# A new order of work at the five sub-layer transitions of a hybrid encoder trunk: uL's first half ahead of the residual, silu between the halves of the second tile's uH, last casts ahead of the last silu

## The chip, the cores and the metric

The kernel runs on one core of one Trainium2 chip. The metric is the device time of one execution in microseconds; it is given as the median of three runs. The profile is of one further execution.

## The reference

Two layers, each a SwiGLU FFN, a token mixer and a second FFN, over x of 256 tokens by 1024 features. Every sub-layer ends in a residual, a layer norm, and the next sub-layer begins with a second standardisation and an adaLN shift and scale:

```python
u = modulate(x, shift, scale)            # standardize(x) * (1 + scale) + shift
f = (silu(g) * up) @ w_ffn_out           # g, up = split(u @ w_ffn_in), 1024 -> 2 x 2816
x = layer_norm(ALPHA * x + 0.5 * (1 + gate) * f, ln_g, ln_b)
u = modulate(x, ...)
m = hybrid_mixer(u, ...)                 # SSD heads beside differential attention, one w_in, one w_out
x = layer_norm(ALPHA * x + (1 + gate) * m, ln_g, ln_b)
u = modulate(x, ...)
f = swiglu(u, ...)
x = layer_norm(ALPHA * x + 0.5 * (1 + gate) * f, ln_g, ln_b)
```

## The kernel before

All products with weights are made in float32 precision from pairs: an operand a is split into a high part (a cast to the type fp32r, on ACT) and a low part (the rest, a subtraction on DVE), and each product is three matmuls (high by high, high by low, low by high). Activations u live in `uH` and `uL`, turned so that features lie on partitions; weights are loaded in halves of 128 by 1024 elements into nine `raw` buffers, cast by `hi_step` and completed by `step` (a low part, plus the next load).

The 256 tokens are two tiles of 128. An FFN runs over eleven blocks of 256 hidden columns; the out-products of a block are made one block later, and for the last four blocks those of tile 1 are kept back. Between two sub-layers stands `cross`: it finishes tile 0 (chain `c0`) and tile 1 (chain `c1`), both by the generator `finish`, while PE makes the kept-back out-products of tile 1 and then the first products of the next sub-layer with tile 0. The order there is written out by hand, in one list for each kind of transition: FFN to mixer (twice, layers 0 and 1), mixer to FFN (twice), FFN to FFN (once, between the layers). Within `cross` DVE, ACT and PE keep exactly the order of the program. The tokens of a list:

- `d0` to `d3`: kept-back out-products; `h`: one cast of a weight half (ACT); `l`: one low part of a weight half (DVE).
- `0 mean`, `0 acc`, `0 rstd`, `0 squares`, `0 rstd2`, `0 turn`: stages of tile 0's chain up to that name. `gate` to `mean` is gate and residual (DVE), `acc` the sums of squares (ACT) and the gamma product (DVE), `squares` the residual stream's new value `xs` (two DVE instructions) and the second sums of squares (ACT), `turn` the normalised `xn` (DVE) and its eight transposes `ptp` (PE). The same with 1 for tile 1.
- `0 us`, `0 u`: the first and the second four features of uH by ACT; `0 m0`, `0 m1`: the unsplit value `um` of each half, again by ACT; `0 l0`, `0 l1` (or a bare `0`, which runs the chain to its end): the subtraction that gives that half of uL, by DVE.
- `P23 1 47`: first products of column blocks 2 and 3 with part 1 and feature blocks 4 to 7. Part 0 is uH by high weights, part 1 uL by high weights, part 2 uH by low weights. Column blocks 0 and 1 share one PSUM bank, 2 and 3 another.
- `e`: evacuation of the first bank. Before a mixer it is one copy on ACT; before an FFN it is `evac`: silu on ACT (tile `sga`), then a product on DVE (tile `hfa`).

After `cross`, tile 1's products with the same weights follow (`mm_a` in an FFN); its first needs a PSUM bank which `e` has emptied. Outside `cross` a scheduler orders instructions within each engine by the dependences.

Of the kernel before, what the change touches and what calls it, by code (L numbers as in the profile page):

```python
# [15 lines left out]
AF = mybir.ActivationFunctionType  # L16
# [11 lines left out]
BC = 256  # L28
NB = DFF // BC
# [16 lines left out]
PRE = 2  # L46
MIX_ADA = (0, 0)
FFN_TO_MIX = ("d0,l,h,d1,d2,d3,0 mean,0 acc,0 rstd,h,h,0 squares,h,l,0 rstd2,h,0 turn,1 gate,1 gate,0 us,0 u,1 mean,"
              "1 acc,P01 02 07,l,1 rstd,0 m0,1 squares,P2 0 07,P2 2 03,P3 0 03,0 l0,P01 1 03,P23 1 03,P3 0 47,1 rstd2,0 m1,"
              "1 turn,0,P01 1 47,1 us,1 u,l,P2 2 47,P23 1 47,l,l,e,P3 2 07,1,h,h,h").split(",")  # L50
MIX_TO_FFN = ("l,d0,h,h,d1,d2,d3,0 mean,h,0 acc,0 rstd,0 squares,l,0 rstd2,h,0 turn,1 gate,1 gate,0 us,0 u,1 mean,"
              "1 acc,P01 02 07,l,1 rstd,0 m0,1 squares,h,P2 0 07,P2 2 03,P3 0 03,0 l0,P01 1 03,P23 1 03,P3 0 47,1 rstd2,0 m1,"
              "1 turn,0,P01 1 47,1 us,1 u,l,P2 2 47,P23 1 47,l,l,e,P3 2 07,1,h").split(",")
FFN_TO_FFN = ("h,l,d0,0 mean,d1,0 acc,0 rstd,h,h,d2,d3,0 squares,l,0 rstd2,h,l,h,h,0 turn,1 gate,1 gate,0 us,0 u,1 mean,"
              "1 acc,P01 02 07,l,1 rstd,0 m0,1 squares,P2 0 07,P2 2 03,P3 0 03,0 l0,P01 1 03,P23 1 03,P2 2 47,P3 0 47,"
              "1 rstd2,0 m1,1 turn,0,P01 1 47,1 us,1 u,l,l,e,P23 1 47,P3 2 07,1,h").split(",")
ORDERS = {"x": FFN_TO_MIX, "m": MIX_TO_FFN, "f": FFN_TO_FFN}

MIX = ("st 1,qk 0 1,ev 1 0,rope 0 0,st 1,small,ev 0 1,tqk 0 0,qk 1 1,rope 1 0,ev 1 1,st 1,st 1,st 1,st 2,st 1,"
# [10 lines left out]
def kernel(  # L70
# [44 lines left out]
    V, S, PE = Queue(nc.vector), Queue(nc.scalar), Queue(nc.tensor)  # L115

    def in_order(on, pe=False):
        V.strict = S.strict = on
        PE.strict = on and pe
# [21 lines left out]
    def gps(name):  # L141
        return pgu.tile([P, 512], F32, tag="gu", name=name)
# [7 lines left out]
    def f(ap):  # L150
        return ap.bitcast(F32)
# [6 lines left out]
    def split(src, hi, lo):  # L158
        S.copy(hi, src)
        V.tensor_tensor(lo, src, f(hi), op=ALU.subtract)  # L160
# [26 lines left out]
    pos = {"load": 0, "hi": 0, "lo": 0}  # L187
    raws, tiles, done = {}, {}, {}
# [6 lines left out]
    def issue_loads(upto):  # L195
        while pos["load"] < min(upto, 2 * len(items)):
            n = pos["load"]
            i, h = divmod(n, 2)
            kind, key, src = items[i]
            if kind == "pair":  # L200
                half = src[h].rearrange("(k p) c -> p k c", p=P)
            else:
                half = src.rearrange("(h k p) c -> h p k c", h=2, p=P)[h]
            shape = {"cols": [4, BC], "pair": [4, BC], "adh": [2, 512]}.get(kind, [1, D])
            raw = rp.tile([P] + shape, F32, tag="raw", name=f"raw_{key}_{h}")
            nc.sync.dma_start(raw, half)
            raws[n] = raw[:, 0, :] if shape[0] == 1 else raw
            pos["load"] += 1
# [13 lines left out]
    def hi_step():  # L222
        n = pos["hi"]
        i, h = divmod(n, 2)
        kind, key, _ = items[i]
        if kind in ADA:
            return False
        issue_loads(n + 1)
        shape = [D] if kind == "rows" else [4, BC]
        ht, lt = [wtile(shape, f"{e}{key}_{h}", F32R) for e in "hl"]  # L230
        tiles.setdefault((kind, key), []).append((ht, lt))
        keep(S.copy(ht, raws[n]), "a")
        pos["hi"] += 1
        return True
# [6 lines left out]
    def step(n=1):  # L241
        for _ in range(n):
            k = pos["lo"]
            if k >= 2 * len(items):
                return
            i, h = divmod(k, 2)
            kind, key, _ = items[i]
            issue_loads(k + 1)
            if kind in ADA:
                pos["hi"] = max(pos["hi"], k + 1)  # L250
                {"ada": ada_step, "adh": adh_step}[kind](key, raws.pop(k), h)
            else:
                if pos["hi"] <= k:
                    hi_step()
                ht, lt = tiles[kind, key][h]
                keep(V.tensor_tensor(lt, raws.pop(k), f(ht), op=ALU.subtract), "v")
            pos["lo"] += 1
            issue_loads(k + 1 + AHEAD)

    stream = {}  # L260

    def order(ins, name):
        tc.add_manual_dep(ins.ins, name, mybir.DependencyInfo(
            mybir.DependencyClass.NoSync, mybir.DependencyReason.SCHED_ONLY), reason="order of issue")

    def keep(ins, e):
        stream[e] = ins.ins.name
        q = V if e == "v" else S
        if q.last and not q.strict:
            order(ins, q.last)  # L270

    def upto(kind, key):
        step(done[kind, key] - pos["lo"])
# [5 lines left out]
    def flush():  # L279
        while late:  # L280
            late.pop(0)()
# [225 lines left out]
    def ln_rows(l, s):  # L507
        lg = wtile([D], f"lg{l}_{s}")
        nc.sync.dma_start(lg, ln_g[l, s].partition_broadcast(P))
        lb = wtile([D], f"lb{l}_{s}")  # L510
        nc.sync.dma_start(lb, ln_b[l, s].partition_broadcast(P))
        slb = sm.tile([P, 1], F32, tag="slb", name=f"slb{l}_{s}", bufs=2)
        S.activation(lb, lb, AF.Identity, accum_out=slb)
        return lg, lb, slb
# [96 lines left out]
    def form_b(o, w, j):  # L611
        sl = slice(j * P, (j + 1) * P)
        for kt in range(KT):
            wh, wl = w[kt // 4]
            mm3(o, wh[:, kt % 4, sl], wl[:, kt % 4, sl], uH[:, :, kt, :], uL[:, :, kt, :], kt == 0, kt == KT - 1)
# [24 lines left out]
    class Ffn:  # L640
# [41 lines left out]

        def evac(self, o, name):
            sg = tp.tile([P, BC], F32, tag="sg", name="sg" + name)
            S.activation(sg, o[:, 0:BC], AF.Silu)
            hf = tp.tile([P, BC], F32, tag="hf", name="hf" + name)
            V.tensor_tensor(hf, o[:, BC:2 * BC], sg, op=ALU.mult)
            return hf
# [144 lines left out]
        def blocks(self, nxt):  # L833
            upto("rows", f"o{self.nm}_{0}")
            for b in range(NA - 1):
                for j in range(2):
                    self.out_both(b, j)
            rows = None
            for b in range(NA, NB):
                step(self.mark[b] - pos["lo"])  # L840
                if self.nm == "00" and b == NA + 2:
                    setup_mixer()
                w = self.weights(b)
                self.htile(b)
                if b == NB - 1:
                    rows = ln_rows(self.l, self.s)
                    target = done["rows", f"o{self.nm}_{b}"] + (PRE if nxt else 0)
                else:
                    target = self.mark[b + 1]
                for j in range(2):  # L850
                    step((target - pos["lo"] + 1 - j) // (2 - j))
                    o = gps(f"ob{self.nm}_{b}{j}")
                    form_b(o[:, 0:BC], w[0], j)
                    form_b(o[:, BC:2 * BC], w[1], j)
                    self.out_both(b - 1, j)
                    hf = self.evac(o, f"b{self.nm}_{b}{j}")
                    hH, hL = self.hts[b]
                    split(hf, hH[:, j, :], hL[:, j, :])
                    flush()
            for h in range(2):  # L860
                for j in range(2):
                    self.out_mm(0, NB - 1, j, (h,))
            defer = [lambda b=b: [self.out_mm(1, b, j) for j in range(2)] for b in range(NB - NDEF, NB - 1)]
            defer.append(lambda: [self.out_mm(1, NB - 1, j, (h,)) for h in range(2) for j in range(2)])
            if nxt is None:
                defer = [lambda h=h: [self.out_mm(1, b, j, (h,)) for b in range(NB - NDEF, NB) for j in range(2)]
                         for h in range(2)]
            cross(self.l, self.s, self.accs, rows, nxt, defer)
# [531 lines left out]
```

## Time and profile before

| quantity | value |
|---|---|
| median of three runs | 1075.6 us (1075.52 to 1075.69) |
| the profiled execution | 1074.92 us, of which the span of the trace is 1073.2 us |
| PE busy in the span | 1031.1 us, 96% |
| DVE, ACT, POOL busy | 825.4, 580.9, 36.1 us (77%, 54%, 3%) |
| mean share of the DMA engines by the hardware queue | 69.6% |

PE is busy all along but for the start, the end and short stretches at the five transitions. A wait in a row stands in brackets behind the instruction that ended it, with the instruction that released it.

### The profile page before, as it was taken

The numbers are of one execution on the slowest core, as the hardware profiler recorded it, in microseconds if no ns is written. First come the engines' busy times: TensorE is split into PE (matmuls) and PEld (weight loads), VectorE is DVE, ScalarE is ACT, GpSimd is POOL, SyncE is SP. The second block draws the span as 40 slices with busy tenths as digits, with TensorE's granted clock in tenths as the row PEclk, the third lists the DMA queues.
The fourth block names the chain that finished last, engine by engine and source line by source line (L and its number), as shares of the span: only waits on it lengthen the run. The fifth ranks groups of instructions, "written<-read, shape, count | busy, mean of one in ns | idle before, by whom it ended". The sixth has DMA issues, their size and how long they took to land.

```text
span 1073.2 us, 19053 instructions
## 1 busy us (share of the span) xinstructions
PE 1031.1 (96%) x7433; PEld 944.3 (88%) x7433; DVE 825.4 (77%) x1284; ACT 580.9 (54%) x1046; POOL 36.1 (3%) x79
## 2 busy tenths in 40 slices
PE   4999999989999999999999999999999999999996
PEld 2899999879897899999989999998899879999995
DVE  5788699688998798768588868847899878756454
ACT  3474434378756755343477433536876578535241
POOL 0000000010000100000010000000000010000000
PEclk9999999999999999999999999999999999999998
DMA  9989799948456389879547979883664628866411
GB/s 341 319 298 370 273 306 407 306 138 254 134 188 225 99 304 341 286 294 361 199 138 249 335 296 377 282 280 107 199 209 150 213 91 302 282 221 216 158 41 39
DMA packets 162559, 258.25 MB, mean 241 GB/s; under 512 B 10807, under 2 KB 125983, under 8 KB 162469
## 3 DMA queue, kind: packets, MB, share of 16 engines
q1 hardware_dynamic: 162468, 257.04, 69.6%
q8 instruction: 58, 0.95, 0.4%
q14 instruction: 33, 0.26, 0.1%
HBM read 255.96 MB, written 1.05 MB: 239 GB/s over the span
## 4 chain that ended last, share of the span: by engine, by line
PE 77%; DVE 10%; ACT 7%; issue 3%; DMA 2%; POOL 1%; SPq 0%; DVEq 0%; POOLq 0%; ACTq 0%
PE ob L108 38%; PE acc L108 18%; PE oa L108 5%; PE ocx L108 2%; PE accx L108 2%; PE ovx L108 2%; DVE xs L108 2%; ACT uH L108 2%; ACT um L108 1%; PE oqkx L108 1%; PE ozx L108 1%; ACT junk L108 1%; DVE acc L108 1%; PE pr L108 1%; DVE lg L108 1%
## 5 line engine op out<-in xcount | busy, mean ns | idle before, releaser
L108 PE MATMUL ob<-uH,hg 128*128 128x256 f32 x576 | 162.6, 282 | 0.0
L108 PE MATMUL ob<-uL,hg 128*128 128x256 f32 x576 | 162.2, 282 | 0.0
L108 PE MATMUL ob<-uH,lg 128*128 128x256 f32 x576 | 161.8, 281 | 0.3 <-DVE lg L108 0.3
L108 PE MATMUL ob<-uH,lu 128*128 128x256 f32 x576 | 162.0, 281 | 0.0
L108 PE MATMUL ob<-uH,hu 128*128 128x256 f32 x576 | 161.9, 281 | 0.0
L108 PE MATMUL ob<-uL,hu 128*128 128x256 f32 x576 | 161.7, 281 | 0.0
L108 PE MATMUL acc<-ho,hH 128*128 128x512 f32 x352 | 137.5, 392 | 1.0 <-ACT ho L108 1.0
L108 PE MATMUL acc<-lo,hH 128*128 128x512 f32 x352 | 137.8, 391 | 0.7 <-DVE lo L108 0.7
L108 PE MATMUL acc<-ho,hL 128*128 128x512 f32 x352 | 137.2, 390 | 0.0
L108 ACT ACTIVATE sgb<-ob 128x256 f32<-128x256 f32 x72 | 27.6, 383 | 202.2 <-PE ob L108 201.8
L108 DVE TENSOR_TENSOR lo<-raw_o,ho 128x1024 fp32r<-128x1024 f32 x88 | 105.6, 1220 | 14.4 <-ACT ho L108 7.2
L108 PEld LDWEIGHTS ob<-uH,hg 128*128 128x128 f32 x576 | 108.3, 188 | 6.2 <-issue 2.5
L108 PEld LDWEIGHTS ob<-uH,lu 128*128 128x128 f32 x576 | 110.1, 191 | 1.2 <-issue 1.2
L108 PEld LDWEIGHTS ob<-uH,lg 128*128 128x128 f32 x576 | 110.2, 191 | 0.6 <-DVE lg L108 0.5
L108 PEld LDWEIGHTS ob<-uL,hg 128*128 128x128 f32 x576 | 108.1, 188 | 2.5
L108 DVE TENSOR_TENSOR lg<-raw_g,hg 128x1024 fp32r<-128x1024 f32 x84 | 101.2, 1221 | 11.2 <-ACT hg L108 5.6
L108 PEld LDWEIGHTS ob<-uH,hu 128*128 128x128 f32 x576 | 108.4, 188 | 0.5 <-issue 0.4
L108 PEld LDWEIGHTS ob<-uL,hu 128*128 128x128 f32 x576 | 108.1, 188 | 0.0
L108 DVE TENSOR_TENSOR lu<-raw_u,hu 128x1024 fp32r<-128x1024 f32 x84 | 100.3, 1219 | 3.4 <-PE ob L108 1.7
L108 ACT CAST hg<-raw_g 128x1024 fp32r<-128x1024 f32 x84 | 86.9, 1056 | 28.1 <-PE acc L108 17.8
L108 DVE TENSOR_TENSOR hfb<-ob,sgb 128x256 f32<-128x256 f32 x72 | 30.3, 420 | 91.2 <-ACT sgb L108 91.0
L108 ACT CAST ho<-raw_o 128x1024 fp32r<-128x1024 f32 x88 | 90.2, 1049 | 12.7 <-PE ob L108 9.0
(535 smaller groups left out, 2307.1 us busy)
## 6 DMA issues: line engine op xcount, KB each, us to landing
raw_o<-in_w_ffn_out_dram SPq DMA_DIRECT2D x88, 512.0 KB, 5.8
raw_g<-in_w_ffn_in_dram SPq DMA_DIRECT2D x84, 512.0 KB, 5.6
raw_u<-in_w_ffn_in_dram SPq DMA_DIRECT2D x84, 512.0 KB, 6.1
raw<-in_w_ffn_in_dram SPq DMA_DIRECT2D x8, 512.0 KB, 8.1
lg<-in_ln_g_dram SPq DMA_DIRECT2D x6, 512.0 KB, 6.0
lb<-in_ln_b_dram SPq DMA_DIRECT2D x6, 512.0 KB
raw_qk0x<-in_w_in_dram SPq DMA_DIRECT2D x4, 512.0 KB, 3.6
raw_qk1x<-in_w_in_dram SPq DMA_DIRECT2D x4, 512.0 KB
```

Of the source, the lines that this page charges most:

```text
L108: ins = emit(*args, **kwargs)
```

## The change

Three things move; no arithmetic changes, and no instruction is added or removed.

1. In all three lists `0 l0` (uL's first half of tile 0, DVE) stands ahead of `1 squares` (tile 1's `xs`) where it stood behind it. PE's uH products `P3 0 47` (four matmuls, in the FFN-to-FFN list also `P2 2 47`) move ahead of the first uL products. In the mixer-to-FFN list one cast `h` moves from behind `1 squares` to ahead of `0 turn`.
2. In all three lists `e` moves from behind the low parts of the weights to a place between `1 us` and `1 u`, that is between the two halves of tile 1's uH on ACT, and ahead of the tokens `l` on DVE.
3. In the first FFN alone (`nm == "00"`) all casts and low parts of the last out-weights are asked for before the last block's first half, its last silu is ordered behind the last of these casts, and the two steps for the next sub-layer (`PRE`) come after the last split, from where on the program's order holds.

```diff
-FFN_TO_MIX: ...1 acc,P01 02 07,l,1 rstd,0 m0,1 squares,P2 0 07,P2 2 03,P3 0 03,0 l0,P01 1 03,P23 1 03,P3 0 47,1 rstd2,0 m1,
-            1 turn,0,P01 1 47,1 us,1 u,l,P2 2 47,P23 1 47,l,l,e,P3 2 07,1,h,h,h
+FFN_TO_MIX: ...1 acc,P01 02 07,l,1 rstd,0 m0,0 l0,1 squares,P2 0 07,P2 2 03,P3 0 07,P01 1 03,P23 1 03,1 rstd2,0 m1,
+            1 turn,0,P01 1 47,1 us,e,1 u,l,P2 2 47,P23 1 47,l,l,P3 2 07,1,h,h,h
-MIX_TO_FFN: ...l,0 rstd2,h,0 turn,...,1 rstd,0 m0,1 squares,h,P2 0 07,P2 2 03,P3 0 03,0 l0,P01 1 03,P23 1 03,P3 0 47,1 rstd2,0 m1,
-            1 turn,0,P01 1 47,1 us,1 u,l,P2 2 47,P23 1 47,l,l,e,P3 2 07,1,h
+MIX_TO_FFN: ...l,0 rstd2,h,h,0 turn,...,1 rstd,0 m0,0 l0,1 squares,P2 0 07,P2 2 03,P3 0 07,P01 1 03,P23 1 03,1 rstd2,0 m1,
+            1 turn,0,P01 1 47,1 us,e,1 u,l,P2 2 47,P23 1 47,l,l,P3 2 07,1,h
-FFN_TO_FFN: ...1 rstd,0 m0,1 squares,P2 0 07,P2 2 03,P3 0 03,0 l0,P01 1 03,P23 1 03,P2 2 47,P3 0 47,
-            1 rstd2,0 m1,1 turn,0,P01 1 47,1 us,1 u,l,l,e,P23 1 47,P3 2 07,1,h
+FFN_TO_FFN: ...1 rstd,0 m0,0 l0,1 squares,P2 0 07,P2 2 07,P3 0 07,P01 1 03,P23 1 03,
+            1 rstd2,0 m1,1 turn,0,P01 1 47,1 us,e,1 u,l,l,P23 1 47,P3 2 07,1,h
 evac:
-            S.activation(sg, o[:, 0:BC], AF.Silu)
+            self.silu = S.activation(sg, o[:, 0:BC], AF.Silu)
 blocks:
-                    target = done["rows", f"o{self.nm}_{b}"] + (PRE if nxt else 0)
+                    target = done["rows", f"o{self.nm}_{b}"] + (PRE if nxt and self.nm != "00" else 0)
-                    step((target - pos["lo"] + 1 - j) // (2 - j))
+                    step(target - pos["lo"] if j or (self.nm == "00" and b == NB - 1) else (target - pos["lo"] + 1) // 2)
+                    cast = stream["a"] if j == 0 else cast
                     hf = self.evac(o, f"b{self.nm}_{b}{j}")
+                    ends = self.nm == "00" and b == NB - 1 and j == 1
+                    if ends:
+                        order(self.silu, cast)
+                        in_order(True)
                     split(hf, hH[:, j, :], hL[:, j, :])
+                    if ends:
+                        step(PRE)
```

## Rows read from the trace of the kernel before

**Rows 1.** The page: busy time by engine.

```profile
PE 1031.1 (96%) x7433; PEld 944.3 (88%) x7433; DVE 825.4 (77%) x1284; ACT 580.9 (54%) x1046; POOL 36.1 (3%) x79
```

**Rows 2.** The chain that ended last: start, duration, what.

```profile
390.97 5.65 PE ob L108 x48
```

**Rows 3.** Waits of PE: in total, times, longest, us.

```profile
PE oa L108 <- DVE uL L108: 4.2, 6, 1.4
PE oqkx L108 <- DVE uL L108: 3.6, 4, 1.6
```

**Rows 4.** Timeline, end of the first FFN: start, duration, engine, instruction [idle before].

```profile
212.87 1.99 ACT L108 CAST ho<-raw_o 128x1024 fp32r<-128x1024 f32 x2
...
213.94 2.36 DVE L108 TENSOR_TENSOR lo<-raw_o,ho 128x1024 fp32r<-128x1024 f32 x2 [0.52 <-ACT ho L108]
...
213.97 0.73 PE L108 MATMUL acc<-ho,hH 128*128 128x512 f32 x2 [0.98 <-ACT ho L108]
...
215.72 1.05 ACT L108 ACTIVATE lb<-lb 128x1024 f32<-128x1024 f32 x1
...
220.11 0.69 DVE L108 TENSOR_TENSOR acc<-acc,gate 128x512 f32<-128x512 f32 x1
...
229.21 1.00 DVE L108 TENSOR_SCALAR xn<-xs,nmqp,rmp 128x512 f32<-128x512 f32 x2 [0.69 <-POOL rmp L182]
...
229.90 1.09 PE L108 MATMUL ptp<-ident,xn 128*128 128x128 f32 x8 [0.79 <-DVE xn L108]
```

**Rows 5.** Timeline, first transition from mixer to FFN.

```profile
356.80 2.90 ACT L108 ACTIVATE uH<-ptp,mod 128x128 fp32r<-128x128 f32 x8 [2.96 <-PE ptp L108]
...
361.15 1.48 ACT L108 ACTIVATE um<-ptp,mod 128x128 f32<-128x128 f32 x4
...
362.22 1.41 DVE L108 SCALAR_TENSOR_TENSOR xs<-accx,rp,lb 128x512 f32<-128x512 f32 x2 [0.60 <-POOL rp L182]
...
363.54 0.68 DVE L108 TENSOR_TENSOR uL<-um,uH 128x512 fp32r<-128x512 f32 x1
...
365.68 1.00 DVE L108 TENSOR_SCALAR xn<-xs,nmqp,rmp 128x512 f32<-128x512 f32 x2 [0.69 <-POOL rmp L182]
...
366.74 1.05 PE L108 MATMUL ptp<-ident,xn 128*128 128x128 f32 x8
...
367.38 2.90 ACT L108 ACTIVATE uH<-ptp,mod 128x128 fp32r<-128x128 f32 x8 [0.30 <-PE ptp L108]
...
367.72 1.22 DVE L108 TENSOR_TENSOR lg<-raw_g,hg 128x1024 fp32r<-128x1024 f32 x1
...
368.86 2.36 DVE L108 TENSOR_TENSOR lu<-raw_u,hu 128x1024 fp32r<-128x1024 f32 x2
...
369.00 0.74 PE L108 MATMUL oa<-lg,uH 128*128 128x256 f32 x4
...
370.30 1.28 ACT L108 ACT_TABLE_LOAD   x1
...
372.01 0.42 DVE L108 TENSOR_TENSOR hfa<-oa,sga 128x256 f32<-128x256 f32 x1 [0.79 <-ACT sga L108]
...
372.49 1.21 PE L108 MATMUL oa<-hg,uH 128*128 128x256 f32 x8 [0.48 <-DVE hfa L108]
...
376.12 1.10 PE L108 MATMUL oa<-hu,uH 128*128 128x256 f32 x8
```

**Rows 6.** Timeline, the transition from FFN to FFN.

```profile
564.07 2.35 DVE L108 TENSOR_TENSOR lu<-raw_u,hu 128x1024 fp32r<-128x1024 f32 x2
...
564.62 2.90 ACT L108 ACTIVATE uH<-ptp,mod 128x128 fp32r<-128x128 f32 x8 [1.62 <-PE ptp L108]
...
568.30 1.21 PE L108 MATMUL oa<-hg,uH 128*128 128x256 f32 x8 [0.46 <-DVE hfa L108]
```

**Rows 7.** Busy time by stretch: us (instructions) of PE, PEld, DVE, ACT, POOL; PE clock; DMA.

```profile
20.00:25.00 5.00, 1.02 (x8) 0.97 (x8) 3.39 (x9) 2.54 (x6) 0.00 (x0) 0.80 1.07 398
25.00:30.00 5.00, 4.50 (x20) 3.68 (x20) 4.52 (x5) 3.81 (x5) 0.00 (x0) 0.52 0.97 346
```

More of the change, by code (lines that the diff above doesn't have):

```diff
@@ L48 @@
 FFN_TO_MIX = ("d0,l,h,d1,d2,d3,0 mean,0 acc,0 rstd,h,h,0 squares,h,l,0 rstd2,h,0 turn,1 gate,1 gate,0 us,0 u,1 mean,"
[L49 to L53, printed above, removed]
+              "1 acc,P01 02 07,l,1 rstd,0 m0,0 l0,1 squares,P2 0 07,P2 2 03,P3 0 07,P01 1 03,P23 1 03,1 rstd2,0 m1,"
+              "1 turn,0,P01 1 47,1 us,e,1 u,l,P2 2 47,P23 1 47,l,l,P3 2 07,1,h,h,h").split(",")
+MIX_TO_FFN = ("l,d0,h,h,d1,d2,d3,0 mean,h,0 acc,0 rstd,0 squares,l,0 rstd2,h,h,0 turn,1 gate,1 gate,0 us,0 u,1 mean,"
+              "1 acc,P01 02 07,l,1 rstd,0 m0,0 l0,1 squares,P2 0 07,P2 2 03,P3 0 07,P01 1 03,P23 1 03,1 rstd2,0 m1,"
+              "1 turn,0,P01 1 47,1 us,e,1 u,l,P2 2 47,P23 1 47,l,l,P3 2 07,1,h").split(",")
 FFN_TO_FFN = ("h,l,d0,0 mean,d1,0 acc,0 rstd,h,h,d2,d3,0 squares,l,0 rstd2,h,l,h,h,0 turn,1 gate,1 gate,0 us,0 u,1 mean,"
-              "1 acc,P01 02 07,l,1 rstd,0 m0,1 squares,P2 0 07,P2 2 03,P3 0 03,0 l0,P01 1 03,P23 1 03,P2 2 47,P3 0 47,"
-              "1 rstd2,0 m1,1 turn,0,P01 1 47,1 us,1 u,l,l,e,P23 1 47,P3 2 07,1,h").split(",")
+              "1 acc,P01 02 07,l,1 rstd,0 m0,0 l0,1 squares,P2 0 07,P2 2 07,P3 0 07,P01 1 03,P23 1 03,"
+              "1 rstd2,0 m1,1 turn,0,P01 1 47,1 us,e,1 u,l,l,P23 1 47,P3 2 07,1,h").split(",")
 ORDERS = {"x": FFN_TO_MIX, "m": MIX_TO_FFN, "f": FFN_TO_FFN}
```

## The prediction

> **What bounds the kernel now.** I read the page first: PE is busy for 1031.1 of 1073.2 us [rows 1], so what can be won is PE's waiting. The view of PE's waits says where it is: the products with uL wait for DVE, 4.2 us before FFNs and 3.6 us before mixers [rows 3]. In order of time these are two waits at each transition: one for uL's first half of tile 0 (1.0 to 1.6 us, 6.0 us over the five) and one for tile 1's uL (0.2 to 0.5 us). The three transitions into an FFN add a wait for `hfa` of 0.2 to 0.5 us [rows 5, 6], and the end of the first FFN adds waits for the last out-weights and for `xn` [rows 4]. All of it is some 11 us, 1%. The chain of waits, and then the timeline of each transition, show what stands behind: DVE and ACT work through tile 1's chain (`xs`, sums, `xn`, uH, um, uL) while PE fills the time with tile 0's products. So the question at each place is whether PE or tile 1's chain comes last.
>
> That is read at `ptp`, tile 1's eight transposes. Where PE waited for `xn`, the transposes began 0.69 us after its start, 229.21 to 229.90 [rows 4]. In the first mixer-to-FFN transition `xn` starts at 365.68, so PE could have transposed from 366.37 and did so at 366.74 [rows 5]: a reserve of 0.37. The same pair of rows stands in all five transitions and gives, in their order, 0.37, 0.37, 0.75, 0.37 and 0.09 us. A wait taken out ahead of `ptp` is therefore worth at most 2.0 us in all, not 6.0; the rest becomes a wait for `xn`.
>
> **Part 1, uL's first half ahead of `xs`.** A product occupies PE for 0.118 us (5.65 us for 48) [rows 2], so the four moved ones cover 0.47 us, the eight 0.94, and they are as long where they are taken away. The subtraction takes DVE some 0.61 us from start to next start and needs `um`, which ACT ends at 361.15 + 1.48 = 362.63; `xs` was free to start at 362.22 [rows 5]. DVE works in order, so `xs` now waits behind the subtraction until 362.65 + 0.61 = 363.27, and with it the sums, `rstd2` and `xn` come 1.05 us later. The five transitions, by the same two rows: 0.4, 1.05, 0.75, 1.1 and 0.8 to 1.05 us. Less the reserve, `ptp` comes 0.05, 0.7, 0.0, 0.75 and 0.7 us later than before, although PE has finished the uL products earlier. The cast moved ahead of `0 turn` falls where ACT stood idle for 2.96 us [rows 5] and costs nothing; without that cover it is 0.95 us on tile 0's uH. It frees ACT for the second `um`, which then no longer holds the second half of uL; that one now follows `xn`.
>
> **Part 2, silu amid uH.** Before a mixer `e` is one copy on ACT. It needs the first bank, which PE ends shortly before the first half of uH is done; um comes at the same distance as before. I add 0.25 us for uL's second half behind `xn`, and carry on to tile 1: +0.3 us (layer 0) and +1.0 us (layer 1).
>
> Before an FFN `e` also puts `hfa` into DVE's order, and behind it now stand `l,l,l`, the low parts that PE's `P2 2 47` and `P3 2 07` need; behind those stand tile 1's uL. Before, they ran while ACT made uH: lg at 367.72, the two lu from 368.86, and only then `hfa` at 372.01 [rows 5]. Walked forward for the first mixer-to-FFN transition: uH starts at 367.38 + 0.7 = 368.05, its first half takes 1.45 (half of 2.90), so 369.5; the table load of 1.28 stands in front of silu, 370.8; silu to `hfa` is 0.43 (371.58 to 372.01), 371.25; `hfa` holds DVE 0.34, 371.6; lg 1.13, and PE may start `P2 2 47` at 372.85, where it started at 369.00. PE has nothing else: its order is fixed too, and the first bank is done by 369.6. Then lu twice, 375.0; the last four products 375.1 to 375.6; tile 1's first product at 375.6 instead of 372.49, that is 3.1 us later. Of this, what tile 1 lost behind it comes back: from 372.49 to 376.12 stand 24 products, 2.83 us, and two transposes, 0.25, so 0.55 us of waiting for uL that has time now. Net +2.55 us. If tile 1's chain were not late (part 1 harmless) it would be +1.9; +2.8 if nothing came back but half. The second mixer-to-FFN transition has the same rows and the same sum.
>
> Between the FFNs silu needs no table load: uH from 564.62, unchanged by the 0.0 above, silu after PE's first bank at 566.2, `hfa` to 567.0, lu twice to 569.25 where they were done at 566.4 [rows 6]; last products to 569.85, against 568.30 for tile 1's first product: +1.55, less 0.55 that comes back, +1.0 us (0.3 to 1.5).
>
> Here a rule speaks against the change. The load of 1.28 us at 370.30 is followed by `hfa` 0.43 us after its end [rows 5], so nothing stands between load and silu. The Trainium skill (ScalarE: Activation LUTs, What ACT_TABLE_LOAD costs) gives a switch of tables 1.28 us and a drain of 1.38 more. By that page silu would come 1.4 us later still in the two transitions and the sum be 2.8 us higher; this trace shows no drain, and I follow the trace.
>
> **Part 3, the last casts.** Before, both casts stood behind the last silu on ACT, at 212.87, both low parts followed from 213.94, and PE waited at 213.97 [rows 4]. The casts go to ACT's idle stretch ahead of that silu, and the low parts to DVE's beside them; the loads that wait for their `raw` buffers start earlier by as much, behind the two layer-norm loads on SP. DVE's order behind the last split is then three low parts, first the two of `PRE`, where it was five. Two low parts and their wait, 2 x 1.14 + 0.5, bring tile 0's gate product from 220.11 to 217.35; if the activation of `lb` at 215.72 (1.05 us) stays between the casts, to 218.1. `xn` follows, and PE, whose own waits there (0.98 and its followers) vanish too, starts the transposes 2.0 to 2.75 us before 229.90. I take 2.2, nearer to the case in which `lb` stays. Should ACT take `lb` ahead of the last silu, its load would hold both, and 0.6 us would be left of it.
>
> **The sum.** FFN to mixer, layer 0: -2.2 + 0.3 = -1.9; mixer to FFN: 2 x 2.55 = +5.1; FFN to FFN: +1.0; FFN to mixer, layer 1: +1.0. In all +5.2 us. The blocks behind each transition hold PE without a wait, so nothing there takes it up. Against the profiled execution's 1074.92 us that is 1080.1; the median of the runs is 0.7 us above that execution, so 1080.8. From the bounds (first FFN, first mixer's transition, mixer to FFN, FFN to FFN, second mixer's): -2.75 + 0.05 + 3.8 + 0.3 + 0.3 = +1.7 at the one end, -0.6 + 0.3 + 5.6 + 1.5 + 1.1 = +7.9 at the other: 1077.3 to 1083.5 for this case.
>
> **Rivals.** *The silu does no harm* (the low parts are not late for PE, because DVE takes them ahead of `hfa` after all, or has done them before). For it: DVE had 0.79 us idle ahead of `hfa`. Against it: their order in the program, which DVE kept in every row of `cross`. Then only part 1's lateness is left: 0.65 for each mixer-to-FFN transition, 0.25 between the FFNs, 1.0 and -1.9: +0.65, or 1076.3.
>
> *Faster.* Tile 1's chain is not the bound, and PE's waits go as meant. It decides at `xn`: it would have to start about 1 us earlier than part 1 puts it, `um` being ready before `xs` may start. Then up to 2.0 us of reserve are won, 2.2 at the first FFN and the 1.1 us of waits for `hfa`: 1070.5. The rows of `um` against `xs` speak against it.
>
> *The clock falls.* Waits of over 3 us with little PE work around them come up only in the two mixer-to-FFN transitions of the changed kernel. Once before, PE did 1.02 us of work in 5 us, and the granted clock went from 1.0 to 0.5, 2.4 to 1.2 GHz, and stayed there over the next 4.5 us of products (0.52) [rows 7]: 4.5 x 0.48 = 2.2 us a fall, so 1083.0 or 1085.2. Against it: there are some 2 us of products just ahead. The Trainium skill (TensorE: Matmul & The Clock Gate, HAM oscillation) tells of the same: waits between bursts put the clock down, and the next burst starts at half speed; rows 7 agree.
>
> **Chances.** A measurement here tells apart some 0.2%, 2.15 us: slower is above 1077.8, faster below 1073.4. The forecast has 62 in 100, the fall of the clock 18, the harmless silu 12, faster 8. So slower 0.80 (the first two), same 0.12, faster 0.08. The range: from under the harmless silu, 1075.5, up to one fall of the clock with some late terms, 1084.0; faster and two falls are left out, some 15 in 100.
>
> **What will show it.** Right: `lg` and `lu` behind `hfa` on DVE in three transitions, PE's waits there now for `lg` and `lu` (3 us once in each mixer-to-FFN transition), waits for `xn` ahead of `ptp`, no wait for `ho`, gate product of the first FFN at 217 to 218 us, and PE's busy time unchanged. Wrong: `xn` no later than before against `um`, or `l` ahead of `hfa`; a clock below 1.0 at a transition would be the third rival.

## The result and the profile after

The changed kernel takes 1084.2 us (median of 4 runs, 1082.3 to 1085.1) where the kernel before takes 1075.6 on the same chip: 1.0083 times as long, 95% interval 1.0064 to 1.0101. A second series gave 1082.4 us (6 runs) against 1074.75, 1.0073 (1.0059 to 1.0088). The forecast was slower, 1080.8, range up to 1084.0: the sign came, the size was 1.6 to 3.4 us short, and the first median lies just above the range.

The page of the changed kernel answers to [rows 1] with this line (busy us, share of the span of 1083.1 us, instructions), and the view of PE's waits to [rows 3] with those under it:

```profile
PE 1036.7 (96%) x7433; PEld 950.8 (88%) x7433; DVE 824.7 (76%) x1284; ACT 581.0 (54%) x1046; POOL 38.4 (4%) x79
```

```profile
PE ptp L108 <- DVE xn L108: 10.4, 6, 1.9
...
PE oa L108 <- DVE hfa L108: 3.6, 2, 2.2
...
PE acc L108 <- ACT hH L108: 1.8, 1, 1.8
```

The waits for uL are gone from the top, as meant. In their place stand waits for `xn` ahead of tile 1's transposes and for `hfa`, and one for `hH` that the forecast did not have. PE's busy time has grown by 5.6 us although no product was added: some of its products ran at the lower clock.

The turns are named here in their order: x0 (FFN to mixer, layer 0), m0 (mixer to FFN), f (FFN to FFN), x1, m1. In the timeline of m0, which answers to [rows 5], start, duration, engine, instruction and, in brackets, the idle time before it read:

```profile
364.40 0.69 DVE L108 TENSOR_TENSOR uL<-um,uH 128x512 fp32r<-128x512 f32 x1 [1.07 <-ACT um L108]
365.01 1.40 DVE L108 SCALAR_TENSOR_TENSOR xs<-accx,rp,lb 128x512 f32<-128x512 f32 x2
...
368.47 1.00 DVE L108 TENSOR_SCALAR xn<-xs,nmqp,rmp 128x512 f32<-128x512 f32 x2 [0.69 <-POOL rmp L182]
369.16 1.24 PE L108 MATMUL ptp<-ident,xn 128*128 128x128 f32 x8 [1.85 <-DVE xn L108]
...
371.35 1.28 ACT L108 ACT_TABLE_LOAD   x1
...
372.64 0.38 ACT L108 ACTIVATE sga<-oa 128x256 f32<-128x256 f32 x1
372.93 1.50 ACT L108 ACTIVATE uH<-ptp,mod 128x128 fp32r<-128x128 f32 x4
373.06 0.42 DVE L108 TENSOR_TENSOR hfa<-oa,sga 128x256 f32<-128x256 f32 x1 [2.99 <-ACT sga L108]
373.40 1.22 DVE L108 TENSOR_TENSOR lg<-raw_g,hg 128x1024 fp32r<-128x1024 f32 x1
373.54 2.07 PE L108 MATMUL oa<-hg,uH 128*128 128x256 f32 x8 [1.34 <-DVE hfa L108]
...
374.53 2.35 DVE L108 TENSOR_TENSOR lu<-raw_u,hu 128x1024 fp32r<-128x1024 f32 x2
375.41 1.48 PE L108 MATMUL oa<-lg,uH 128*128 128x256 f32 x6
```

DVE's order is the forecast's: uL, then `xs`, then `xn`, and `hfa` ahead of `lg` and `lu`. DVE stands idle for 2.99 us in front of `hfa` with `lg` behind it. The silu starts 0.01 us after the load of the table: of the drain that the Trainium skill puts behind it (ScalarE: Activation LUTs, What ACT_TABLE_LOAD costs) this trace shows nothing either. PE's row at 373.54 is what the forecast did not have: these are tile 1's products with the high parts, which PE takes before `lg` is there. So within `cross` PE keeps the order of the list among the list's own products only: these, which the program has behind `cross`, came in between. Eight of them last 2.07 us where [rows 5] has 1.21.

The busy time by stretch (columns as in [rows 7]) shows why:

```profile
360.00:370.00 10.00, 8.14 (x71) 7.93 (x69) 7.01 (x18) 7.53 (x22) 2.43 (x5) 1.00 0.17 53
370.00:377.00 7.00, 5.66 (x28) 5.25 (x27) 4.01 (x6) 6.97 (x18) 0.00 (x0) 0.52 0.17 50
...
762.00:770.00 8.00, 7.33 (x39) 6.99 (x39) 5.71 (x12) 6.51 (x18) 0.00 (x0) 0.57 0.61 184
...
895.00:899.00 4.00, 4.00 (x23) 3.95 (x22) 3.90 (x6) 3.82 (x10) 0.00 (x0) 0.58 0.58 184
```

The third column from the end is the granted clock: 0.52 to 0.58 over the three stretches behind m0, x1 and m1, so for most of each it stood at the lower of its two levels, 1.2 GHz. By the clock's record in the trace that was 6.83, 6.83 and 3.41 us. The text calls such a stretch a fall of the clock. The profile of the kernel before has none at a turn.

The end of the first FFN, which answers to [rows 4]:

```profile
213.62 0.39 ACT L108 ACTIVATE sgb<-ob 128x256 f32<-128x256 f32 x1 [3.74 <-PE ob L108]
...
216.56 1.06 ACT L108 ACTIVATE lb<-lb 128x1024 f32<-128x1024 f32 x1 [2.56 <-DMA lb<-in_ln_b_dram]
...
217.62 0.39 ACT L108 CAST hH<-hfb 128x256 fp32r<-128x256 f32 x1
...
218.06 0.50 PE L108 MATMUL acc<-ho,hH 128*128 128x512 f32 x1 [1.77 <-ACT hH L108]
...
222.40 0.69 DVE L108 TENSOR_TENSOR acc<-acc,gate 128x512 f32<-128x512 f32 x1
...
232.25 1.08 PE L108 MATMUL ptp<-ident,xn 128*128 128x128 f32 x8 [1.64 <-DVE xn L108]
```

The casts of `ho` are done ahead of the last silu as meant. But ACT now takes the pass over `lb` between silu and the copy `hH`, waits 2.56 us there for the transfer of `lb`, and PE waits 1.77 us for `hH`.

### The profile page after: what moved, and what is told of

The parts are those of the page before. It is cut to its first block, busy times and chain, and to the rows that moved or that the text cites. A ratio compares the mean times of both kernels' runs of the same rounds, so it can differ in the third digit from the quotient of the medians.

```text
span 1083.1 us, 19061 instructions
## 1 busy us (share of the span) xinstructions
PE 1036.7 (96%) x7433; PEld 950.8 (88%) x7433; DVE 824.7 (76%) x1284; ACT 581.0 (54%) x1046; POOL 38.4 (4%) x79
## 4 chain that ended last, share of the span: by engine, by line
PE 81%; DVE 7%; ACT 6%; issue 2%; DMA 2%; POOL 1%; SPq 0%; DVEq 0%; POOLq 0%; ACTq 0%
PE ob L108 37%; PE acc L108 19%; PE oa L108 6%; PE oqkx L108 3%; PE ocx L108 3%; PE accx L108 2%; PE ovx L108 2%; ACT junk L108 2%; DVE xs L108 1%; ACT uH L108 1%; ACT um L108 1%; PE ozx L108 1%; PE pr L108 1%; DMA lb<-in_ln_b_dram 1%; PE psex L108 1%
```

## The experiments

One table for all runs comes first. Each number is the time that a stretch took in that kernel's profile, less the time in the profile of before, by the starts of PE's rows. The stretches: `start` up to the first FFN's last `ob` product; `FFN1 end` up to x0's first transpose; `mixer 0` up to that mixer's first output product; `m0 ptp` up to tile 1's transposes in m0; `m0 rest` up to the next FFN's first `ob`; `f` up to the `ob` after the turn; `x1 ptp` up to tile 1's transposes in x1; `x1 rest` up to a product `scx` 32 us behind them, inside the second mixer; `m1 ptp` and `m1 rest` like those of m0. `sum` is the difference of the whole spans. The last column has the turns with a fall of the clock, and its us.

```
kernel              start FFN1end mixer0 m0ptp m0rest    f  x1ptp x1rest m1ptp m1rest    sum  falls at turns
after                1.93   0.41  -0.64  0.71  2.09 -0.21  0.16  2.56  0.74  2.16   9.91  m0 6.83, x1 6.83, m1 3.41
e1_part1             1.93   0.00  -0.67  0.71 -0.27 -0.17  0.77  0.03  0.72  0.02   3.05  m0 3.41, m1 3.41
e2_part2             2.53   0.00  -0.86 -0.08  2.35 -0.09  0.00  0.01  0.02  1.89   5.76  m1 3.41
e3_part3             1.79   0.32  -0.93  0.00 -0.03 -0.15  0.00  0.00  0.01  0.01   1.00  x0 3.41
e4_parts12           1.59  -0.01  -0.69  0.70  2.73  0.13  0.77  1.51  0.56  0.63   7.90  m0 3.41, x1 3.41
e5_all               1.68  -0.42  -0.72  0.69  2.55 -0.24  0.76  1.39  0.70  0.65   7.03  m0 6.83, x1 3.41
e6_all_lb            0.43  -2.02  -0.67  0.69  2.45 -0.26  0.15  0.19  0.64  0.62   2.21  none
e7_all_split         0.21   0.82  -0.68  0.69  0.00 -0.25  0.77  2.67  0.65  0.03   4.90  FFN1 end 3.41, x1 6.83
e8_all_warm          0.12  -0.03  -0.65  0.70  2.34 -0.27  0.15  0.09  0.70  0.68   3.81  none
e9_part3_lb         -0.03  -2.02  -0.53  0.02 -0.01 -0.25 -0.61  0.02  0.01  0.02  -3.37  none
e10_part3_lb_split   0.78  -2.03  -0.83  0.00  0.01 -0.29 -0.61  0.03  0.00 -0.23  -3.20  none
e11_all_mended       0.84  -2.00  -0.62  0.71  0.01 -0.22  0.16  0.10  0.59  0.06  -0.38  none
e12_part3_lb_start  -1.27  -2.07   1.94  0.02 -0.01 -0.59 -0.61  0.02  0.02  0.06  -2.51  none (mixer 0 3.41)
```

Three columns carry noise. `start` differs by up to 2.6 us between kernels with the same code there. It goes mostly with the cold stretch at about 22 us, which lasts 6.83 us in before, e6 to e10 and 10.24 us in the others (none in e12). `mixer 0` is 0.5 to 0.9 us shorter than in the one profile of before wherever its clock held, whatever was changed. `x1 ptp` has a third FFN in front of it that took 0.61 us less in seven of the profiles, so 0.15 there is 0.76 of the turn.

**e1, part 1 alone.** The lists get the early `0 l0`, the eight products and the cast; `e` stays. The list into an FFN, for one:

```diff
-... 0 squares,l,0 rstd2,h,0 turn, ... 1 rstd,0 m0,1 squares,h,P2 0 07,P2 2 03,P3 0 03,0 l0,P01 1 03,P23 1 03,P3 0 47,1 rstd2
+... 0 squares,l,0 rstd2,h,h,0 turn, ... 1 rstd,0 m0,0 l0,1 squares,P2 0 07,P2 2 03,P3 0 07,P01 1 03,P23 1 03,1 rstd2
```

> Part 1 alone (uL's first half ahead of xs, the uH products and one cast moved; e and the first FFN as before). Theory order (tile 1's chain is late behind the subtraction, and PE waits for xn ahead of the transposes): ptp is late by 0.05, 0.7, 0.0, 0.75 and 0.7 us in the five transitions, some +2 us in all, PE waiting 1.4 to 1.9 us for xn in each, and the clock stays at 1.0. Theory clock (the waits also put PE's clock to half): in addition falls at two or three transitions at 1.5 to 2.4 us each, +5 us or more. Theory gain (the change's own aim): the 6.0 us of waits for uL go and nothing comes: -5 us.

1077.8 us, 1.0025 (1.0016 to 1.0034). `ptp` is 0.71, 0.77 and 0.72 us late in m0, x1 and m1, and no other column but the noise of `start` is late. The waits are for `xn` (in m0 1.84 us). The lateness of part 1 was forecast at 0.7, 0.75 and 0.7 us. The theory of the clock is half right here: it fell at m0 and m1 for 3.41 us each, but the rests behind, -0.27 and 0.02 us, show no cost.

**e2, part 2 alone.** Only `e` is moved:

```diff
-"1 turn,0,P01 1 47,1 us,1 u,l,P2 2 47,P23 1 47,l,l,e,P3 2 07,1,h"
+"1 turn,0,P01 1 47,1 us,e,1 u,l,P2 2 47,P23 1 47,l,l,P3 2 07,1,h"
```

> Part 2 alone (silu between the halves of tile 1's uH). Theory order as predicted (low parts behind hfa, PE has nothing else to do): +1.9 us in each mixer-to-FFN transition, +1.5 between the FFNs, about 0 before mixers: +5 us. Theory order as amended by the changed kernel's trace (tile 1's high products are put into the wait): 0 to +1.5 us in all. Theory clock: falls only in the mixer-to-FFN transitions, if at all, +1.5 us each.

1079.2 us, 1.0032 (1.0020 to 1.0045). m0 costs 2.35 us with no fall of the clock, m1 1.89 with one, the turns f, x0 and x1 nothing: less than +5 us in all, more than the amended theory allowed. In m0 DVE stands idle 2.73 us in front of `hfa` and PE waits 1.94 us for it.

**e3, part 3 alone.** The first FFN's end as in the change, the lists as before:

```diff
-step((target - pos["lo"] + 1 - j) // (2 - j))
+step(target - pos["lo"] if j or (self.nm == "00" and b == NB - 1) else (target - pos["lo"] + 1) // 2)
...
+if ends:
+    order(self.silu, cast)
+    in_order(True)
```

> Part 3 alone (first FFN). Theory lb (ACT takes the activation of lb ahead of the last copy hH and waits there for lb's load): PE waits some 1.8 us for hH instead of for ho, ptp of the first transition comes 0.5 us later than before, and the total is within 1 us of before. Predicted in its place: 2.2 us faster.

1074.9 us, 0.9996 (0.9987 to 1.0004): the gain of 2.2 us that the forecast gave to part 3 is not there.

**e4, parts 1 and 2 together.** The lists of the change, the first FFN as before.

> Parts 1 and 2 without part 3. If part 3 is worth nothing, this has the changed kernel's time, +8 to +9 us. Theory order alone: +2.5 to +3 us with a clock of 1.0 at all transitions. Theory clock: the difference to that is in stretches at 1.2 GHz, one at each of two to three transitions, and the mean granted clock is 0.984 to 0.988 against 0.994 before.

1080.4 us, 1.0051 (1.0037 to 1.0064), 5.3 us above before, so neither the 8 to 9 of the whole change nor the 2.5 to 3 of the order alone. m0 costs 3.4 us and m1 1.2; x1 has a fall of the clock and takes 1.51 us more behind `ptp`, where e1 has none and takes 0.03.

**e5, the change once more,** beside the three kernels that take one suspect out of it.

> The changed kernel itself, a second time, on one chip with the three kernels below. Two theories of why the three parts together cost more than parts 1 and 2 and part 3 one by one (+5.3 and -0.2 us). Clock theory: the order of work costs as much as in those runs, and the rest is the clock, which falls to its lower level at more transitions when all three parts are in; the profile then shows falls around the transitions beside the one at the start, each worth about 1.5 us per 3.4 us at the lower level, and the time is 1082 to 1085. Rival: the first execution profile was unlucky and the sum is that of the parts, 1080 to 1081, with one fall or none.

1082.4 us, 1.0073 (1.0059 to 1.0088), with falls at m0 and x1. The ten runs of both series lie between 1080.6 and 1085.1, all above e4's median. The mean granted clock was 0.983 to 0.990 in them and 0.988 to 0.992 in e4's: the theory of the clock fits, and the sum of parts alone is too low.

**e6, the change with `lb` out of the way.** In the first FFN `ln_rows` now leaves out ACT's pass over `lb`; the line behind `step(PRE)` makes it instead.

```diff
-rows = ln_rows(self.l, self.s)
+rows = ln_rows(self.l, self.s, self.nm != "00")
...
 if ends:
     step(PRE)
+    S.activation(rows[1], rows[1], AF.Identity, accum_out=rows[2])
```

> The changed kernel with one edit at the end of the first FFN: ACT's pass over lb is issued behind the last casts and can no longer stand between the last silu and the copy hH. Theory (lb is why part 3 won nothing): the gate product of the first FFN's end comes at 217.5 to 218.5 us instead of 222.4 (relative to a start as late as in that profile add up to 1.9), the wait of 1.77 us for hH is gone, tile 0's transposes begin 2 to 4 us earlier than in the changed kernel, and the time is 2 us below e5. Rival: the products gain, but the first mixer gives it back, because its start is set by another engine: its output products are no earlier than in e5 and the time is within 0.5 us of e5. Second rival: xn still waits for lb through the gate and nothing moves at all.

1078.6 us, 1.0037 (1.0024 to 1.0050), 3.8 us below e5. The timeline of the first FFN's end:

```profile
212.12 0.38 ACT L108 ACTIVATE sgb<-ob 128x256 f32<-128x256 f32 x1 [3.74 <-PE ob L108]
...
213.00 0.41 ACT L108 CAST hH<-hfb 128x256 fp32r<-128x256 f32 x1 [0.49 <-DVE hfb L108]
...
215.21 1.05 ACT L108 ACTIVATE lb<-lb 128x1024 f32<-128x1024 f32 x1
...
218.47 0.69 DVE L108 TENSOR_TENSOR acc<-acc,gate 128x512 f32<-128x512 f32 x1
...
228.32 1.08 PE L108 MATMUL ptp<-ident,xn 128*128 128x128 f32 x8 [1.29 <-DVE xn L108]
```

`hH` follows the silu by 0.88 us instead of 4.00, the gate product stands at 218.47, and the stretch is 2.02 us shorter than in before. Nothing takes that up. The order in m0 is still the change's, so this clean profile also shows what follows there:

```profile
369.55 1.32 PE L108 MATMUL oa<-hg,uH 128*128 128x256 f32 x8 [2.20 <-DVE hfa L108]
...
385.33 1.05 ACT L108 CAST hg<-raw_g 128x1024 fp32r<-128x1024 f32 x1 [2.92 <-DMA raw_g<-in_w_ffn_in_dram]
386.28 0.64 ACT L108 CAST hH<-ph 128x256 fp32r<-128x256 f32 x2
...
386.97 0.51 PE L108 MATMUL acc<-ho,hH 128*128 128x512 f32 x1 [1.32 <-ACT hH L108]
```

After m0 ACT has the copies `hH` behind a cast that waits 2.92 us for its weights, and PE waits 1.32 us more, 17 us after the turn. In the kernel before the copies stand ahead of that cast, and PE does not wait; the same stretch of its timeline:

```profile
385.08 0.64 ACT L108 CAST hH<-ph 128x256 fp32r<-128x256 f32 x2
...
386.04 1.05 ACT L108 CAST hg<-raw_g 128x1024 fp32r<-128x1024 f32 x1 [0.31 <-DMA raw_g<-in_w_ffn_in_dram]
```

m1 has the same 2.20 us wait for `hfa` at 888.04 and no second one; its rest costs 0.62 us where m0's costs 2.45.

**e7, the change with `hfa` back behind the low parts;** the silu stays amid uH. The new token `v` is DVE's product:

```diff
-"1 turn,0,P01 1 47,1 us,e,1 u,l,P2 2 47,P23 1 47,l,l,P3 2 07,1,h"
+"1 turn,0,P01 1 47,1 us,e,1 u,l,P2 2 47,P23 1 47,l,l,v,P3 2 07,1,h"
```

> The changed kernel with the silu where the change put it on ACT, amid uH, but its product on DVE behind the second and third low part, where it stood before. Theory (what costs in the turns into an FFN is hfa standing ahead of the low parts in DVE's order): lg starts about 1.8 us earlier against uH, PE's wait of 1.3 to 1.9 us for hfa at the first tile-1 product is below 0.5, the two mixer-to-FFN turns cost 0.4 and 0.7 us as with part 1 alone instead of 2.3 to 2.8, and the time is 3.5 to 4.5 us below e5, about 1080. Rival: the silu itself and its table load amid uH are the cost (1.28 us and 0.4 us put in front of uH's second half, um and xn): then the turns stay as dear and the time is within 1 us of e5.

1078.0 us, 1.0030 (1.0018 to 1.0042), 4.4 us below e5. m0 behind `ptp`:

```profile
368.62 1.22 DVE L108 TENSOR_TENSOR lg<-raw_g,hg 128x1024 fp32r<-128x1024 f32 x1
...
369.89 0.74 PE L108 MATMUL oa<-lg,uH 128*128 128x256 f32 x4
369.98 1.28 ACT L108 ACT_TABLE_LOAD   x1
...
372.02 0.42 DVE L108 TENSOR_TENSOR hfa<-oa,sga 128x256 f32<-128x256 f32 x1
...
372.74 1.10 PE L108 MATMUL oa<-hg,uH 128*128 128x256 f32 x8
```

The table's load still stands in the middle of uH, and the rest of m0 and m1 costs 0.00 and 0.03 us. So the early silu is harmless and its product in DVE's order was the cost. x1 fell to the lower clock for 6.83 us in this profile and lost 2.67 us.

**e8, the change with products that nobody reads** (86 in all, by [rows 2] 0.118 us each, in PE's order at the five turns). `w10` issues ten into a bank of their own:

```diff
-... P2 2 03,P3 0 07,P01 1 03,P23 1 03,1 rstd2,0 m1,1 turn,0,P01 1 47,1 us,e, ...
+... P2 2 03,P3 0 07,P01 1 03,P23 1 03,w10,1 rstd2,0 m1,1 turn,0,P01 1 47,w14,1 us,e, ...
```

> The changed kernel with products that nobody reads put into PE's order where it waits at the end of each transition: ten ahead of tile 1's transposes, and four (into an FFN fourteen in the mixer-to-FFN list) behind them; 0.118 us each. They are extra work; everything else is unchanged. Theory (clock): with PE kept busy there the granted clock stays at its upper level at the transitions, and the time is 2 to 4 us below e5 although PE does 3 to 4 us more of work that fills waits. Rival (order): the clock matters little, the products that do not fit into the waits add their time, and the kernel is as slow as e5 or slower by up to 2 us.

1080.0 us, 1.0049 (1.0035 to 1.0062): 86 x 0.118 = 10 us more of PE's work and 2.4 us less time than e5. The mean granted clock of its six runs is 0.992 to 0.994, where e5 has 0.983 to 0.990. The profile has no fall at a turn (m0, then x1, by stretch):

```profile
370.00:377.00 7.00, 6.45 (x54) 6.20 (x53) 6.13 (x7) 6.99 (x18) 0.00 (x0) 1.00 0.48 143
...
762.00:770.00 8.00, 7.79 (x65) 7.43 (x64) 6.55 (x12) 8.00 (x17) 0.00 (x0) 1.00 0.84 243
```

x1's rest goes from 1.39 us in e5 to 0.09, while m0's 2.34 and m1's 0.68 stay: those are the order's, not the clock's.

**e9, part 3 with `lb` out of the way, on the lists of before.** e3 with the edit of e6.

> Part 3 alone with ACT's pass over lb issued behind the last casts; the three lists as before. Theory (lb between silu and hH is what cost part 3 its gain): the first FFN's end is 2.0 to 2.7 us earlier against its last ob product, as in e6, nothing takes it up, and the time is 1072.5 to 1073.5 where the kernel before has about 1075. Rival (the gain is given back later): the mixer or a turn behind it takes the gain up and the time is within 0.7 us of before.

1072.1 us, 0.9978 (0.9967 to 0.9989). `FFN1 end` is 2.02 us shorter and keeps it to the end. This version beats both kernels, by 0.2% the one before; its code is the kernel before, part 3 and the edit of e6.

**e10, e9 with the silu amid uH** and its product where `e` stood.

```diff
-"1 turn,0,P01 1 47,1 us,1 u,l,P2 2 47,P23 1 47,l,l,e,P3 2 07,1,h"
+"1 turn,0,P01 1 47,1 us,e,1 u,l,P2 2 47,P23 1 47,l,l,v,P3 2 07,1,h"
```

> e9 with one edit in the lists of before: silu (the copy before a mixer) amid tile 1's uH as in the change, its product on DVE where e stood, behind the low parts; parts 1 and the moved products stay undone. Theory (in the changed lists only the product's place did harm, the early silu itself helps): PE's waits for hfa of 0.5 and 0.2 us ahead of tile 1's products go and the time is 0.5 to 1 us below e9. Rival (silu and its table load of 1.28 us in front of uH's second half cost as much as they give): um and xn are late by it, the waits turn into waits for uL, and the time is within 0.4 us of e9 or above it.

1072.3 us, 0.9981 (0.9972 to 0.9990), the same as e9: the rival holds. By the view of PE's waits, 1.4 us of waiting for `hfa` are gone and the waits for uL ahead of FFN products have grown from 4.1 to 5.3 us.

**e11, the change with all three mended:** e6 and e7 together, and ten unread products ahead of tile 1's transposes at each turn, four behind them at x0, m0, x1 and m1.

> The changed kernel with all three suspects taken out together: lb behind the last casts, the product hfa behind the low parts, and unread products (ten ahead of tile 1's transposes, four behind them before a mixer and in the turns into an FFN from a mixer) to keep the clock up. If order, lb and clock are the whole of what the change cost, the rest is the lateness of xn from part 1, 0.7 us at three turns, less 2.0 to 2.7 at the first FFN: 1074.5 to 1075.5, the same as before. If something of the change is still unnamed, it stays above 1076.5.

1075.2 us, 1.0003 (0.9993 to 1.0013), as the sum of the named terms gave. What is left of the change is part 1's lateness, 0.71, 0.76 and 0.59 us, against the 2.00 us of the first FFN.

**e12, e9 with twenty unread products at the start,** in PE's two waits ahead of the cold stretch of [rows 7].

```diff
-"...,a,a,a,p0,a,p1,h,m,h,h,l,l,..."
+"...,a,a,a,p0,a,w,p1,w,h,m,h,h,l,l,..."
```

> e9 with twenty products that nobody reads in PE's two waits of 2.4 and 2.8 us at the start of the kernel (ten each, ident by ident), just ahead of the stretch of 6.8 to 10.2 us in which the granted clock is 0.5 in every profile so far. Theory (the clock falls on such waits, and each 3.4 us at the lower level cost 1.5 us of a busy PE): the fall at the start is gone, the time is 1.5 to 3 us below e9 and the executions lie closer together. Rival (the start is set by transfers and DVE, the low clock there costs nothing): the fall goes and the time stays within 0.5 us of e9; or the products themselves come late and it is up to 1 us slower.

1072.8 us, 0.9985 (0.9975 to 0.9995), not below e9. The cold stretch at the start is gone; the rows answer to [rows 7], and a third one shows where the clock fell instead:

```profile
20.00:25.00 5.00, 5.00 (x46) 5.00 (x46) 3.40 (x9) 2.58 (x6) 0.00 (x0) 1.00 1.07 398
25.00:30.00 5.00, 4.89 (x33) 3.54 (x33) 4.49 (x5) 3.84 (x5) 0.00 (x0) 1.00 0.98 346
...
270.00:275.00 5.00, 3.43 (x30) 2.94 (x28) 4.84 (x16) 3.71 (x8) 0.00 (x0) 0.86 0.59 197
```

The start is 1.24 us shorter than e9's. In this execution the first mixer then fell to the lower clock for 3.41 us and took 2.5 us more than e9's. That fall is not the whole answer: three of the twelve runs have a mean clock of 0.997, above the 0.996 of this one, and take 1071.4 to 1071.6 us, while e9's four fastest take 1070.2 to 1071.1 at 0.994 to 0.995. Where the start's gain went stays open.

## Why the prediction was right in sign and short in size

**The step that put the time above the range is the clock, which the sum held at nothing.** The forecast spoke against a fall with "there are some 2 us of products just ahead"; it came at three turns all the same, and at x1 and m1 it cost 4.0 us in the profile of after. The order's own sum came out at the 5.2 us forecast, but by luck, since its terms were off in both directions. They follow one by one.

**Part 1: right.** `ptp` late by 0.71, 0.77 and 0.72 us (e1) against 0.7, 0.75 and 0.7, and by nothing at x0 and f. The carried-on costs at x0 and x1 (0.25 us for uL's second half) came in small part or not at all: behind x1's `ptp` e1 has 0.03 us, the kernels with `e` moved too and no fall there (e6, e8, e11) 0.09 to 0.19, and the turn x0 costs nothing.

**Part 2, mixer to FFN: the mechanism right, two sizes off.** `hfa` ahead of the low parts is the cost (e7). The step that failed is "PE has nothing else: its order is fixed too". Behind the lists PE's order is set by the scheduler, and it put tile 1's high products ahead of the blocked low ones: PE's row at 373.54 comes 1.87 us before its first product with `lg`, at 375.41. So the turn itself costs 0.7 us and a rest of 0.62 to 0.68 (m1 of e4, e5, e6, e8), 1.3 to 1.4 us, half of the 2.55. m0 costs 0.7 and 2.3 to 2.5 us, 3.1 in all. Of its extra 1.8 us, 1.32 are the wait for `hH` at 386.97 in e6; the forecast ended its walk some 10 us earlier, at the row 376.12 of [rows 5]. That the order on ACT there changed with the position of `hfa` is read from e7, where `hH` and m0 are right again; which rule of the scheduler did it was not tried.

**Part 2, FFN to FFN: missed.** +1.0 us was forecast and -0.25 to +0.13 measured (e2, e4, e5), no more than kernels without part 2 differ there. The reason is the same: PE filled the wait with tile 1's products.

**Part 3: mis-sized, by a case close to the one that the text named and did not choose.** The forecast took 2.2 us, for `lb` between the casts, and 0.6 should ACT take `lb` ahead of the last silu. ACT took it just behind that silu, ahead of `hH`, and the stretch changed by -0.42 to +0.41 us (e5, e8, e3, after; e7 lost more to a fall of the clock there). With `lb` kept behind, the 2.0 us are there in every run (e6, e9 to e12).

**The clock: given 18 in 100 as a case of its own; it came in both series.** The size per fall was near (2.2 us by [rows 7]): 3.41 us at the lower clock at x1 cost 1.2 to 1.5 us (e4 and e5 against e1 and e6), 6.83 us 2.4 to 2.6 (after, e7). The place was half wrong. It was sought in the mixer-to-FFN turns for their long waits, and the dearest fall of after is at x1, whose rest grew by 2.56 us. At m0 a fall costs nothing that can be read: 2.09, 2.55 and 2.73 us with it (after, e5, e4), 2.34 to 2.45 without (e2, e6, e8). PE waits for others there anyway. At x1, behind the wait for `xn`, there is no such cover, and at m1 it costs 1.2 to 1.5 us (e2 and after against e4, e5, e6 and e8) where it comes 4 to 6 us behind `ptp`, and nothing (0.02) in e1, where it comes 0.6 us behind it. The forecast's condition, waits of over 3 us, was too strict: x1 fell behind a wait of 1.86 us.

**The sum.** By the profile of after: turns and first FFN by order 0.4 + 2.8 - 0.2 + 0.8 + 1.4 = 5.2 us, where the forecast had 5.2 too, by errors that cancel (m1, f and x1 too dear, m0 and the first FFN too cheap). The rest of the 9.9 us is 4.0 of clock at x1 and m1 and 1.9 at the start, less 0.6 in the first mixer and 0.6 in the third FFN. (The rival *faster* adds up to 1070.3, not the 1070.5 of the text.) The start differs from execution to execution without the change; the clock at x1 and m1 is the change's, since no profile with the lists of before has it.

## What to carry to other kernels

In an order written by hand for several engines, the place of a product on one engine (here `hfa` on DVE) counts more than that of the function ahead of it: moving silu alone cost nothing, moving its product with it some 3 us over two turns (e2 and e4 to e6 against e7). Moving casts ahead of a silu freed ACT for whatever else could run; look at what the engine will take in the gap, and at the transfer that this waits for. A list that fixes the emission does not fix the order behind it: read the order of each engine for the first 20 us after a changed turn, not up to the first product alone.

## What the runs showed of the hardware that was not expected

At x1 the same order of work up to the transposes and the same wait for `xn`, 1.86 or 1.87 us, stand in six profiles. The clock held in e1 and e6, fell for 3.41 us in e4 and e5 and for 6.83 us in after and e7. PE was busy 8.13 of the 10 us around the wait in after (first fence) and 8.14 in e1 (second fence), and there the clock held over the next 8 us too:

```profile
761.86 1.40 PE L108 MATMUL ptp<-ident,xn 128*128 128x128 f32 x8 [1.86 <-DVE xn L108]
...
752.00:762.00 10.00, 8.13 (x70) 7.96 (x68) 6.45 (x17) 8.04 (x22) 2.18 (x5) 1.00 0.20 55
```

```profile
759.68 1.09 PE L108 MATMUL ptp<-ident,xn 128*128 128x128 f32 x8 [1.86 <-DVE xn L108]
...
752.00:762.00 10.00, 8.14 (x67) 7.67 (x66) 6.53 (x12) 7.50 (x21) 2.18 (x5) 1.00 0.19 53
762.00:770.00 8.00, 7.57 (x62) 7.32 (x62) 6.65 (x12) 7.98 (x18) 0.00 (x0) 1.00 0.88 248
```

So the wait makes a fall possible and does not decide it. The Trainium skill (TensorE: Matmul & The Clock Gate, Part 1: The HAM clock gate) says that the chip watches the activity of PE on a count of its own, not tied to the kernel's start, so that one kernel can show different cold stretches from run to run. These six profiles, and the cold start of 6.83 or 10.24 us for the same code, agree with it. Products that nobody reads, 0.118 us each in waits that were there anyway, kept the clock up at every turn of e8 and e11 and cost nothing that can be measured. Why e6, whose turns wait as in e5, has no fall in its profile and a higher mean clock in its runs (0.990 to 0.995 against 0.983 to 0.990) stays open.
